# The weights of the modulation in groups of eight units at every hand-over, two of them ahead of the sums of squares, and the copies that end a group behind later products

## The chip, the cores and the metric

One core of a Trainium2 chip runs the whole program. The metric is the device time of one execution in microseconds; a kernel's time is the median of its runs.

## What is computed

One inference step of a decoder trunk of four layers (width D = 1024, feed-forward width 2816), in float32. 256 prompt tokens and 8 samples of 4 tokens each use the same weights, so the matrices work on 288 columns. The modulation vectors come from the conditions alone (one for the prompt, eight for the samples), so that they can be computed at any time before they are needed:

```
c_act = silu(c)
for i in range(4):                                  # mixers: pool, attention, GLA, pool
    shift1, scale1, gate1, shift2, scale2, gate2 = split(c_act @ w_ada[i] + b_ada[i], 6)
    h = rms_norm(x, norm_gain[i, 0]) * (1 + scale1) + shift1
    x = x + gate1 * mixer(h)                        # mixer i mod 3, with its state or caches
    h = rms_norm(x, norm_gain[i, 1]) * (1 + scale2) + shift2
    x = x + gate2 * conv_ffn(h)                     # up-projection, width-3 conv, gelu gate, down-projection
y = rms_norm(x, final_gain)
```

The pool mixer subtracts tokens from their causal windowed means and multiplies four groups by their own matrices; the attention mixer has three dilation groups merged by their denominators; GLA is gated linear attention in chunks of 64. States and caches are outputs too.

## The kernel before

Activations lie transposed, features on partitions and the 288 tokens on the free axis, in eight tiles of 128 features. A product in float32 is made of three matmuls (`prod`, L386 to L390): weights and activations are each split into a high and a low half, and high x high (L388), high x low (L389) and low x high (L390) are summed in PSUM. The weights are split on the chip: ScalarE copies a half unit into `whi` (L320), VectorE subtracts that from the raw weights into `wlo` (L328).

**Steps and loads.** The whole program is one list of steps, executed by `execute` (L257). A step with a `piece` is a product on half a unit of weights; the splits of its piece are placed ahead of it, up to four pieces (`W_BUFS`), or `ahead` pieces where a step says so. A step with a `unit` reads raw weights. Units are 1 MB (128 x 2048 float32). They are loaded by SyncE (L299) in the order of their use into a ring of six raw buffers (`RAW_BUFS`); a new load is issued when a buffer comes free, that is after the last `wlo` of a weight unit or after the matmuls of a modulation unit. `lows`, the pending `wlo` subtractions, are emitted behind the next step.

**Modulation** (`ada_steps`, L487 to L543). `w_ada` of one layer is 24 units of 1 MB. A group makes two vectors out of eight units, or one vector out of four (`groups` says which: first vector, number). A unit is eight matmuls of 128x512 on the 32 columns of the conditions (L508), summed in one PSUM tile of its own (`adaps`). Behind the last unit of a group come two "busy" steps: `evac`, a copy of that PSUM tile by ScalarE to `adasb` (L518), and `fin`, four transposes on TensorE (ps<-cm,adasb in the rows, by the helper at L384) and the additions on VectorE (L529, L537). Layer 0's units stand in the start of the program and in its mixer. Layers 1 to 3 are computed out of a queue, some of it a layer ahead.

**Where the queue is drained.** The mixers' steps stand in strings written out by hand (`POOL_ORDERS`, `ATTN_ORDER`, `GLA_ORDER`); a "+" is the next step of the queue, be it a unit, an `evac` or a `fin`. In the FFNs `place` (L196) puts units after counted pieces, by `FFN_FILL`: so many units where the first norm is, and then `{piece: units}`. Its `ends` lets the busy steps stand one piece or more behind the last unit. `arrange` (L1961) reads the strings.

**A hand-over.** At the end of each mixer and each FFN the last weight pieces give the eight feature tiles of the residual. `each` (L581) adds a tile into `x` (L596, L598, L600), ScalarE squares it (L556), VectorE adds squares up in `ssq` (L559), and after the last tile two matmuls against a matrix of ones give the sums over the features (`square_add`, L570; sqps<-ssq and sqps<-sq). Then the root (L609 to L616) and the norm, which writes the halves `hh` and `hl` of the next input (L648, L679, L684) that the next products wait for. The modulation units of the hand-over (six of them at most places: `norm + + + + + +`, `begin + + + + + +`) stand between the sums and those products in TensorE's order. In the pool mixer the products are L981 to L983, the means' transposition L1018 to L1022, and its residual has names of its own (`add0`, `squares0`, `add1`, `squares1`).

At the attention layer kr0 transposes probabilities (ps<-cm,P), o-steps accumulate values (acc<-kv,PT), mx and om merge the groups, and w0a to w3b are the output products, with O as what is merged. In GLA fi0 to fi3 make the halves of the output (L1850 to L1852), and w0a to w3b are its output products.

Of the kernel before, what the change touches and what calls it, by code (L numbers as in the profile page):

```python
# [44 lines left out]
norm + + + + + + norm2 gates product0 product1 + + pre ys0 ys1 + + add0 squares0 add1 squares1 end  # L45
# [4 lines left out]
+ + + t0a y1a v0a t0d y1b v0b o0a kr0 t0c s1a y1c wr0 q2a o0b o0c sv0 t1a + + y1d s1b q2b t1b s1c y1e o0d k2a  # L50
y1f y1g s1d k2b t1c t1d + + kr1 v1a y1h sc1 + v1b s2a v2a o1a t2a o1c o1b st1 s2b v2b y2a t2b o1d y2b sv1 sc2
s2c s2d kr2 + wt mu0 om1 t2d mu1 wr2 om0 st2 o2a wr1 mx0 sm1 o2b t2c sm0 mx1 w0a sv2 om2 o2c o2d w1a sm2 mx2 pre + +
+ w0b + w1b + w3a w2a w2b w3b end
# [3 lines left out]
begin + + + + + + q0a q0b gd masks q1a + ga2 ga0 q1b ga1 + k0a cu0 + k0b cu3 k1a cu2 cu1 k1b xs6 xs5 es x0 v0a  # L57
ms5 x1 ks v0b ms7 m0b + m0a v1a x2 ms6 m1a m1b ps m2a up0 v1b v2a x3 uo0 un0a un0c m3a un0b m3b x4 up1 m2b un0d
v2b uo1 m4b v3a un1b x5 m4a + un1a m5a m5b x6 un1c up2 v3b m6a un1d uo2 + un2a m7a m6b un2c r0a en cr kr0 m7b un2b +
un2d r0b kr1 op1 r1a op0 up3 uo3 un3a un3c r1b un3b un3d r2a os op3 op2 sp0 ns0 sp1 si0 ns1 nr0 og1 r2b r3a ns2 ns3 og0 nr1  # L60
r3b fi0 fi1 si1 og2 og3 + pre + + w0a + w1a + fi2 fi3 + + w0b w1b w2a w2b w3a w3b end
"""

FFN_FILL = ((0, {8: 4, 20: 4, 34: 4}), (6, {30: 2}), (6, {16: 2, 34: 4}), (4, {}))
# [106 lines left out]
class Step:  # L171


    __slots__ = ("fn", "piece", "unit", "gap", "busy", "ahead", "key", "need")
# [21 lines left out]
def place(main, queue, first, runs):  # L196


    out, ends = [], []
    queue = list(queue)  # L200
    seen = 0

    def units(n):
        while n:
            s = queue.pop(0)
            n -= not s.busy
            (ends if s.busy else out).append(s)
            if s.busy and len(ends) > 2:
                out.append(ends.pop(0))
        while queue and queue[0].busy:  # L210
            ends.append(queue.pop(0))
    for s in main:
        if s.need is not None:
            if queue and queue[0].key <= s.need:
                raise ValueError(f"late: {queue[0].key}")
            out.append(s)
            units(first)
            continue
        out.append(s)
        if s.piece is not None:  # L220
            seen += 1
            if ends:
                out.append(ends.pop(0))
            if seen in runs:
                units(runs[seen])
    return out, queue


class Trunk:
# [27 lines left out]
    def execute(self, steps):  # L257
# [53 lines left out]
        for kind, v in plan:  # L311
# [20 lines left out]
            else:  # L332
# [154 lines left out]
    def ada_steps(self, l, m0, nm, own=None):  # L487
# [53 lines left out]
        for s in st:  # L541
            s.key = (l, m0)
# [34 lines left out]
    def residuals(self, i, m):  # L577

        sq = [self.ssq]

        def each(t, ps):  # L581
            f, G = 2 * i + t, m()
            if f == 7:
                self.flush(self.adds)
            self.residual_x(ps, f, G)
            self.flush(self.adds)
            sq.append(self.square(f, "later"))
            if f == 7:
                self.square_add(6, self.ssq)
                self.square_add(7, sq[-1])  # L590
        return each
# [482 lines left out]
    def attn_steps(self, l):  # L1074
# [418 lines left out]
        for i in range(4):  # L1493
            put(f"w{i}", self.pair_steps(w_out[:, i * 256:(i + 1) * 256], lambda: (self.hh, self.hl), None, (6,), ((0, 4), (4, 6)),
                                         each=self.residuals(i, lambda: self.mod(l, 2)), ahead=AHEAD if i == 3 else None))
        return T
# [394 lines left out]
    def build(self):  # L1891
# [6 lines left out]
        for n, l in enumerate(Ls):  # L1898
            groups = ((0, 2), (2, 1), (4, 1), (3, 1), (5, 1)) if n == 0 else ((0, 2), (2, 1), (3, 2), (5, 1)) if n == len(Ls) - 1 else ((0, 2), (2, 2), (4, 2))
# [14 lines left out]
        for n, l in enumerate(Ls):  # L1914
            kind = l % 3
            after = None
            if kind == 0:
                if n == 0:
# [3 lines left out]
                    p["product0"].ahead, p["product1"].ahead = 2, 1  # L1922
# [4 lines left out]
                p["pre"] = Step(lambda: self.preload(AF.Abs_reciprocal_sqrt), ahead=None if n else 2)  # L1927
                after = p.pop("outs2")
                m = self.arrange(p, POOL_ORDERS[min(n, 1)], queue)
            else:  # L1930
                m = m2 if kind == 1 else self.gla_steps(l)
                m = self.arrange(m, ATTN_ORDER if kind == 1 else GLA_ORDER, queue)
# [12 lines left out]
            f, queue = place(f, queue, *FFN_FILL[n])  # L1945
# [5 lines left out]
    def arrange(self, named, order, queue):  # L1951

        out = []
        for t in order.split():
            if t != "+":
                s = named.pop(t)
                while s.need is not None and queue and queue[0].key <= s.need:
                    out.append(queue.pop(0))
                out.append(s)
            elif queue:  # L1960
                out.append(queue.pop(0))  # L1961
# [94 lines left out]
```

## Time and profile before

| | |
|---|---|
| median of three runs | 1398.32 us (1393.46, 1398.32, 1399.51) |
| the profiled execution | 1400.07 us |
| its span | 1398.3 us |
| mean granted clock of TensorE | 0.973 |
| HBM read and written | 300.21 MB and 19.76 MB |
| DMA rate over the span | 229 GB/s |

The span is what the profiler saw from the first to the last instruction; the execution's time has 1.8 us more around it. In the page's lines a row is a group of instructions: line, engine, operation, output<-inputs, shapes, number, then busy us and mean ns of one, and behind a second bar the idle time ahead of them and what ended it. DVE is VectorE, ACT ScalarE, POOL GpSimd, SP SyncE, PE TensorE, PEld its loading of weights.

### The profile page before, as it was taken

What the parts mean: (1) busy time and instruction counts of PE and PEld (TensorE: products, weight loads), DVE (VectorE), ACT (ScalarE), POOL (GpSimd) and SP (SyncE); (2) the same over time, 40 slices, a digit from 0 to 9 for tenths busy, and PEclk for the clock granted to TensorE, in tenths of its full rate; (3) what the DMA queues carried; (4) which work ended last, traced back from release to release, by engine and by line L of the source; (5) the groups of instructions that cost most, each with busy time, mean ns of one, the idle gap of its engine ahead of it and who ended that gap; (6) DMA issues with size and microseconds to landing.
All of it is one profiled execution on the core that took longest, in us unless ns stands there. A gap on an engine that the chain in (4) does not pass through costs nothing.

```text
span 1398.3 us, 25411 instructions
## 1 busy us (share of the span) xinstructions
PE 1330.4 (95%) x10075; PEld 1205.3 (86%) x10075; DVE 853.2 (61%) x1673; ACT 641.4 (46%) x1152; POOL 209.4 (15%) x510
## 2 busy tenths in 40 slices
PE   5899999998999999999999999799999999999997
PEld 3479899987786699999978887699999967999997
DVE  2576666446335776674465654676765566777644
ACT  3364445335443555453354336364544344545542
POOL 2220011001001122110034324121100021101100
PEclk8899999999999999999999999999999997999999
DMA  9997866559656796875593476596575577545520
GB/s 344 356 301 267 263 205 218 173 181 341 229 188 215 276 315 228 289 266 172 181 339 101 151 241 223 192 314 232 181 246 173 172 286 239 166 158 165 174 84 34
DMA packets 206231, 310.48 MB, mean 222 GB/s; under 512 B 7692, under 2 KB 186742, under 8 KB 196496
## 3 DMA queue, kind: packets, MB, share of 16 engines
q1 hardware_dynamic: 201296, 286.82, 61.3%
q0 software_dynamic: 4352, 21.50, 4.2%
q8 instruction: 79, 1.29, 0.4%
q10 hardware_dynamic: 464, 0.54, 0.1%
q14 instruction: 40, 0.33, 0.1%
HBM read 300.21 MB, written 19.76 MB: 229 GB/s over the span
## 4 chain that ended last, share of the span: by engine, by line
PE 83%; DVE 6%; DMA 4%; ACT 3%; issue 2%; POOL 1%; SPq 0%; DVEq 0%; ACTq 0%; POOLq 0%
PE mm L388 22%; PE mm L390 22%; PE mm L389 22%; PE adaps L508 4%; DMA raw<-w_ada 3%; PE ps L384 2%; DMA raw<-attn_w_in 1%; PE ps L1625 1%; PE sqps L570 1%; PE mm L758 1%; PE mm L759 1%; PE mm L760 1%; DVE ht L648 1%; DVE hl L684 1%; DVE wlo L328 1%
## 5 line engine op out<-in xcount | busy, mean ns | idle before, releaser
L388 PE MATMUL mm<-hh,whi 128*128 128x288 f32 (+1 forms) x1752 | 524.4, 299 | 3.4 <-ACT hh L679 1.9
L389 PE MATMUL mm<-hl,whi 128*128 128x288 f32 (+1 forms) x1752 | 519.3, 296 | 0.8 <-DVE hl L684 0.6
L390 PE MATMUL mm<-hh,wlo 128*128 128x288 f32 (+1 forms) x1752 | 519.2, 296 | 0.1
L328 DVE TENSOR_TENSOR wlo<-raw,whi 128x1024 fp32r<-128x1024 f32 (+2 forms) x335 | 393.3, 1190 | 152.5 <-ACT whi L320 152.1
L320 ACT ACTIVATE whi<-raw 128x1024 fp32r<-128x1024 f32 (+2 forms) x335 | 343.0, 1028 | 281.5 <-PE mm L389 184.8
L388 PEld LDWEIGHTS mm<-hh,whi 128*128 128x128 f32 (+1 forms) x1752 | 330.9, 189 | 17.0 <-issue 9.2
L389 PEld LDWEIGHTS mm<-hl,whi 128*128 128x128 f32 (+1 forms) x1752 | 330.8, 189 | 1.9 <-POOL hs L671 0.6
L390 PEld LDWEIGHTS mm<-hh,wlo 128*128 128x128 f32 (+1 forms) x1752 | 330.6, 189 | 0.6 <-DVE wlo L328 0.3
L388 PE MATMUL mm<-ah,whi 128*128 128x288 f32 x704 | 208.5, 296 | 0.0
L390 PE MATMUL mm<-ah,wlo 128*128 128x288 f32 x704 | 208.0, 295 | 0.0
L389 PE MATMUL mm<-al,whi 128*128 128x288 f32 x704 | 206.9, 294 | 0.0
L389 PEld LDWEIGHTS mm<-al,whi 128*128 128x128 f32 x704 | 132.8, 189 | 0.0
L388 PEld LDWEIGHTS mm<-ah,whi 128*128 128x128 f32 x704 | 132.5, 188 | 0.0
L390 PEld LDWEIGHTS mm<-ah,wlo 128*128 128x128 f32 x704 | 132.3, 188 | 0.0
L815 DVE TENSOR_SCALAR c<-ext,vec 128x304 f32<-128x304 f32 x88 | 38.7, 439 | 127.3 <-ACT ext L812 124.9
L818 DVE SCALAR_TENSOR_TENSOR c<-ext,vec,c 128x304 f32<-128x304 f32 x176 | 94.9, 539 | 6.3
L508 PE MATMUL adaps<-raw,cT 128*32 128x512 f32 x736 | 92.7, 631 | 5.8 <-DMA raw<-w_ada 5.8
L824 POOL COPY convS<-ext 128x2 f32<-128x2 f32 x88 | 16.2, 184 | 448.7 <-ACT ext L811 448.7
L811 ACT ACTIVATE ext<-mm 128x256 f32<-128x256 f32 x88 | 33.9, 386 | 83.0 <-PE mm L390 83.0
L821 ACT ACTIVATE ge<-c 128x304 f32<-128x304 f32 x88 | 39.9, 458 | 57.4 <-DVE c L818 56.6
L508 PEld LDWEIGHTS adaps<-raw,cT 128*32 128x32 f32 x736 | 20.6, 112 | 52.9 <-issue 39.7
L556 ACT ACTIVATE sq<-x 128x288 f32<-128x288 f32 x63 | 27.7, 444 | 63.5 <-DVE x L600 56.0
(387 smaller groups left out, 1484.6 us busy)
## 6 DMA issues: line engine op xcount, KB each, us to landing
raw<-w_ada SPq DMA_DIRECT2D x92, 1024.0 KB, 5.8
raw<-ffn_w_in SPq DMA_DIRECT2D x80, 1024.0 KB, 8.7
raw<-ffn_w_down SPq DMA_DIRECT2D x32, 1024.0 KB, 5.0
raw<-ffn_w_down SPq DMA_DIRECT2D x16, 768.0 KB, 6.1
raw<-gla_w_in SPq DMA_DIRECT2D x12, 1024.0 KB, 13.4
raw<-ffn_w_in SPq DMA_DIRECT2D x16, 512.0 KB, 6.2
win_s<-cache_win_g POOLq DMA_DIRECT2D x16, 512.0 KB, 4.6
raw<-attn_w_in SPq DMA_DIRECT2D x7, 1024.0 KB
```

The costliest lines, as they stand in the source:

```text
L320: self.nc.scalar.activation(out=hv, in_=r, func=AF.Copy)
L328: self.nc.vector.tensor_tensor(out=lv, in0=r, in1=hv.bitcast(F32), op=ALU.subtract)
L384: self.nc.tensor.transpose(out=out, in_=in_, identity=self.ident[0:k, 0:k])
L388: mmul(out=out, lhsT=wh, rhs=xh, start=start, stop=False)
L389: mmul(out=out, lhsT=wh, rhs=xl, start=False, stop=False)
L390: mmul(out=out, lhsT=wl, rhs=xh, start=False, stop=stop)
L508: nc.tensor.matmul(out=ps[32 * q:32 * q + 32, :], lhsT=self.cT[:, k * per + r, :], rhs=v[:, r, j * 512:(j + 1) * 512], start=(k == 0), sto ...
L556: nc.scalar.activation(out=sq, in_=self.x[:, f, :], func=AF.Square)
L811: nc.scalar.activation(out=e[:, 2:258], in_=ps[t][:, 0:TP], func=AF.Copy)
L815: nc.vector.tensor_scalar(out=c1, in0=e[:, 0:304], scalar1=w[0], scalar2=self.vcol("ffn_conv_b", l * 22 + f), op0=ALU.mult, op1=ALU.add)
L818: nc.vector.scalar_tensor_tensor(out=c1, in0=e[:, k:k + 304], scalar=w[k], in1=c1, op0=ALU.mult, op1=ALU.add)
L821: nc.scalar.activation(out=ge, in_=c1, func=AF.Gelu)
```

## The change

`place` goes, and with it the drawing of units, `evac` and `fin` by separate "+". The new `spread` only puts "+" marks behind counted pieces of an FFN, and the new `fill` goes through the finished list: a "+" takes one unit. When the last unit of a group is taken, its `evac` is put three pieces further on and its `fin` five pieces further on, or ahead of the next group's first unit or of the step that needs the vectors, whichever comes first.

At every hand-over from layer 1 on there are two units ahead of the sums of squares, which are now a step of their own (`self.sums`), and six behind: a whole group of eight. At the last one, into FFN3, four units are left, two ahead of the second half of the sums' steps and two behind. The units in the FFNs of layers 1 to 3 go; in attention and GLA pairs stand at four places each (in attention after kr0, y1g, st1 and o2a; in GLA after x4, pre, w0a and fi3). In layer 3 the order of the groups becomes (0,2), (3,2), (2,1), (5,1), two units stand behind the pool products, and `gates` (which needs the vector of the gate) moves behind the products. Three of attention's steps and the pool's products and `pre` in layer 3 get a smaller `ahead`. The number of units, and every sum, stays. Buffers stay at six. At f == 7 the residual is now added ahead of the pending adds, and the pending `wlo` are emitted ahead of a unit's load.

```
+def spread(main, runs):
+    out = []
+    seen = 0
+    for s in main:
+        out.append(s)
+        if s.piece is not None:
+            seen += 1
+            out.extend("+" * runs.get(seen, 0))
+    return out
+
+def fill(entries, queue):
     out, ends = [], []
     queue = list(queue)
     seen = 0
+    def take():
+        s = queue.pop(0)
+        if s.first:
+            while ends:
+                out.append(ends.pop(0)[1])
+        out.append(s)
+        k = 3
         while queue and queue[0].busy:
+            ends.append((seen + k, queue.pop(0)))
+            k += 2
+    for e in entries:
+        if e == "+":
+            if queue:
+                take()
             continue
+        if e.need is not None:
+            while any(q.key <= e.need for q in queue):
+                take()
+            while any(q.key <= e.need for _, q in ends):
+                out.append(ends.pop(0)[1])
+        out.append(e)
+        if e.piece is not None:
             seen += 1
+            while ends and ends[0][0] <= seen:
+                out.append(ends.pop(0)[1])
...
-norm + + + + + + norm2 gates product0 product1 + + pre ys0 ys1 + + add0 squares0 add1 squares1 end
+norm + + + + + + norm2 product0 product1 + + gates pre ys0 ys1 add0 squares0 add1 + + squares1 end
...
-FFN_FILL = ((0, {8: 4, 20: 4, 34: 4}), (6, {30: 2}), (6, {16: 2, 34: 4}), (4, {}))
+FFN_RUNS = ({8: 4, 20: 4, 34: 4}, {}, {}, {})
...
                     v.fn(*[u.view(raw.pop(u)) for u in v.unit])
+                    flush_lows()
                     for u in v.unit:
...
             f, G = 2 * i + t, m()
-            if f == 7:
-                self.flush(self.adds)
             self.residual_x(ps, f, G)
             self.flush(self.adds)
             sq.append(self.square(f, "later"))
             if f == 7:
-                self.square_add(6, self.ssq)
-                self.square_add(7, sq[-1])
+                def sums():
+                    self.square_add(6, self.ssq)
+                    self.square_add(7, sq[-1])
+                self.sums = sums
...
+            if n and kind == 0:
+                f = list("++") + [f[0]] + list("+" * 6) + f[1:]
+            elif n:
+                f = ["+", "+", Step(lambda: self.sums()), f[0]] + list("+" * 6) + f[1:]
+            if n:
+                m = ["+", "+", Step(lambda: self.sums())] + m
             st += m + f
-        return st
+        return fill(st, queue)
```

How it moves TensorE's instructions at the hand-over from FFN1 to GLA: the last rows of the down-projection (al and ah are its input's halves), the sums, the units (a row of 4 is one unit) and GLA's first product. Before:

```order
L388 MATMUL mm<-ah,whi 128x288
L389 MATMUL mm<-al,whi 128x288
L390 MATMUL mm<-ah,wlo 128x288
L570 MATMUL sqps<-ssq,ones 128x288
L570 MATMUL sqps<-sq,ones 128x288
L508 MATMUL adaps<-raw,cT 32x512 x24
L388 MATMUL mm<-hh,whi 128x288
```

and now, at the same place of the changed kernel, whose lines are some 16 further down:

```order
L404 MATMUL mm<-ah,whi 128x288
L405 MATMUL mm<-al,whi 128x288
L406 MATMUL mm<-ah,wlo 128x288
L524 MATMUL adaps<-raw,cT 32x512 x8
L586 MATMUL sqps<-ssq,ones 128x288
L586 MATMUL sqps<-sq,ones 128x288
L524 MATMUL adaps<-raw,cT 32x512 x24
L404 MATMUL mm<-hh,whi 128x288
```

Two units moved ahead of the two sums, and six are still behind them.

The loads that SyncE issues for that place, in order, before:

```order
L299 DMA raw<-gla_w_in 128x8x256
L299 DMA raw<-w_ada 128x2048 x6
L299 DMA raw<-gla_w_in 128x8x16
L299 DMA raw<-gla_w_in 128x8x256 x2
L299 DMA raw<-w_ada 128x2048
L299 DMA raw<-gla_w_in 128x8x256
```

and now:

```order
L314 DMA raw<-gla_w_in 128x8x256
L314 DMA raw<-w_ada 128x2048 x8
L314 DMA raw<-gla_w_in 128x8x16
L314 DMA raw<-gla_w_in 128x8x256 x7
L314 DMA raw<-state_gla 128x8x256
L314 DMA raw<-w_ada 128x2048 x2
```

Eight loads of w_ada now stand ahead of GLA's next weights, where six stood, and the units that were spread over GLA's start are no longer between its weights.

In attention, on TensorE around kr0 (kT keys, P probabilities and cm the constant used for transposing), before:

```order
L1268 MATMUL acc<-kv,PT 128x64
L384 MATMUL ps<-cm,kT 128x128 x4
L384 MATMUL ps<-cm,kT 32x128 x2
L384 MATMUL ps<-cm,P 128x128 x3
L1227 MATMUL ps<-kT,qT 128x128
```

and now:

```order
L1284 MATMUL acc<-kv,PT 128x64
L400 MATMUL ps<-cm,kT 128x128 x4
L400 MATMUL ps<-cm,kT 32x128 x2
L524 MATMUL adaps<-raw,cT 32x512 x8
L400 MATMUL ps<-cm,P 128x128 x3
L1243 MATMUL ps<-kT,qT 128x128
```

Two units stand between the transposition of the keys and that of the probabilities.

More of the change, by code (lines that the diff above doesn't have):

```diff
@@ L171 @@
 class Step:
-    __slots__ = ("fn", "piece", "unit", "gap", "busy", "ahead", "key", "need")
+    __slots__ = ("fn", "piece", "unit", "gap", "busy", "ahead", "key", "need", "first")
     def __init__(self, fn, piece=None, unit=None, gap=0, busy=False, ahead=None, need=None):
@@ L193, in merge @@
     return out
-def place(main, queue, first, runs):
+def spread(main, runs):
[8 more added lines that the diff above has]
+def fill(entries, queue):
     out, ends = [], []
@@ L201, in place @@
     seen = 0
[L203 to L209, printed above, removed]
-        while queue and queue[0].busy:
[L211 to L217, printed above, removed]
-            continue
-        out.append(s)
-        if s.piece is not None:
-            seen += 1
[L222 to L226, printed above, removed]
+    def take():
[5 more added lines that the diff above has]
+        k = 3
+        while queue and queue[0].busy:
+            ends.append((seen + k, queue.pop(0)))
[4 more added lines that the diff above has]
+                take()
+            continue
+        if e.need is not None:
[5 more added lines that the diff above has]
+        if e.piece is not None:
+            seen += 1
+            while ends and ends[0][0] <= seen:
+                out.append(ends.pop(0)[1])
+    if queue or ends:
+        raise ValueError("units left")
+    return out
 class Trunk:
@@ L540, in ada_steps @@
         st.append(Step(fin, busy=True))
-        for s in st:
-            s.key = (l, m0)
+        for k, s in enumerate(st):
+            s.key, s.first = (l, m0), k == 0
         return st
@@ L1495, in attn_steps @@
                                          each=self.residuals(i, lambda: self.mod(l, 2)), ahead=AHEAD if i == 3 else None))
+        for t in ("v1b", "v2a", "v2b"):
+            T[t].ahead = 2
         return T
@@ L1921, in build @@
                             p[f"b{k}{i}"] = step
-                    p["product0"].ahead, p["product1"].ahead = 2, 1
                     p["root"] = Step(self.root)
@@ L1926, in build @@
                     del p["open"], p["past"], p["room"]
-                p["pre"] = Step(lambda: self.preload(AF.Abs_reciprocal_sqrt), ahead=None if n else 2)
+                p["product0"].ahead, p["product1"].ahead = 2, 1
+                p["pre"] = Step(lambda: self.preload(AF.Abs_reciprocal_sqrt), ahead=2)
                 after = p.pop("outs2")
-                m = self.arrange(p, POOL_ORDERS[min(n, 1)], queue)
+                m = self.arrange(p, POOL_ORDERS[min(n, 1)])
             else:
                 m = m2 if kind == 1 else self.gla_steps(l)
-                m = self.arrange(m, ATTN_ORDER if kind == 1 else GLA_ORDER, queue)
+                m = self.arrange(m, ATTN_ORDER if kind == 1 else GLA_ORDER)
             f = self.ffn_steps(l)
@@ L1944, in build, with arrange @@
                 f.insert(24, m2.pop("lines"))
-            f, queue = place(f, queue, *FFN_FILL[n])
+            f = spread(f, FFN_RUNS[n])
             if kind == 1:
                 f = merge(f, self.copies, 8, len(f) - 26)
-            st += m + f
-        return st
[L1951 to L1961, printed above, removed]
+            if n and kind == 0:
[4 more added lines that the diff above has]
+                m = ["+", "+", Step(lambda: self.sums())] + m
+            st += m + f
+        return fill(st, queue)
+    def arrange(self, named, order):
+        out = [t if t == "+" else named.pop(t) for t in order.split()]
         if named:
```

18 lines of the change are left out of this document (9 added, 9 removed).

## The prediction

> **What bounds the kernel now.** I read the page first: the span, the busy time of the engines, the costliest groups and the DMA issues.
>
> ```profile
> span 1398.3 us, 25411 instructions
> PE 1330.4 (95%) x10075; PEld 1205.3 (86%) x10075; DVE 853.2 (61%) x1673; ACT 641.4 (46%) x1152; POOL 209.4 (15%) x510
> L508 PE MATMUL adaps<-raw,cT 128*32 128x512 f32 x736 | 92.7, 631 | 5.8 <-DMA raw<-w_ada 5.8
> raw<-w_ada SPq DMA_DIRECT2D x92, 1024.0 KB, 5.8
> ```
>
> TensorE is busy 95% of the span, so only two things can move the end: its idle time, some 68 us, and the clock at which it works. The modulation units (L508, 8 matmuls each) are work that can stand anywhere, and a unit's megabyte takes a median of 5.8 us from issue to landing. Next I read TensorE's waits (total, times, longest).
>
> ```profile
> PE ps L384 <- DVE hl L1852: 7.7, 1, 7.7
> PE sqps L570 <- DVE ssq L559: 4.3, 5, 2.5
> PE sqps L570 <- ACT sq L556: 1.7, 5, 0.4
> PE ps L384 <- DVE kv L1205: 1.4, 1, 1.4
> PE ps L384 <- DVE O L1418: 1.1, 1, 1.1
> PE ps L1227 <- ACT KT L1305: 0.7, 1, 0.7
> PE ps L1227 <- ACT PT L1254: 0.5, 1, 0.5
> ```
>
> The largest is at the end of GLA. The two waits of the sums of squares come to 4.3 + 1.7 = 6.0 us. The other four are in attention. Third, the timeline of TensorE at the hand-over from FFN1 to GLA (start, length, idle before in brackets), and SyncE's issues there.
>
> ```profile
> 696.15 0.75 PE L570 MATMUL sqps<-ssq,ones 128*128 128x288 f32 x2 [0.55 <-DVE ssq L559]
> 697.22 0.75 PE L570 MATMUL sqps<-sq,ones 128*128 128x288 f32 x2 [0.31 <-ACT sq L556]
> 697.90 5.36 PE L508 MATMUL adaps<-raw,cT 128*32 128x512 f32 x48
> 703.19 0.40 PE L388 MATMUL mm<-hh,whi 128*128 128x288 f32 x1
> ```
>
> ```profile
> 693.07 0.33 SPq L299 DMA_DIRECT2D raw<-w_ada  x1
> 699.02 2.94 SPq L299 DMA_DIRECT2D raw<-gla_w_in  x3
> ```
>
> Six units run for 5.36 us without a gap while the norm is made, and the first product follows at once. All six were loaded beforehand; the next load is issued at 699.02, that is 1.12 us after the first unit began, when its buffer is free. Last, the windows view, for the clock (columns: from and to, length, busy time of PE, PEld, DVE, ACT, POOL, then PEclk, DMA share, GB/s).
>
> ```profile
> 365.86:369.27 3.41, 2.02 (x16) 1.56 (x16) 2.48 (x4) 0.59 (x2) 0.39 (x1) 1.00 0.03 9
> 369.27:372.68 3.41, 3.41 (x15) 2.76 (x14) 0.81 (x5) 1.82 (x7) 1.54 (x3) 0.50 0.46 175
> 471.67:475.08 3.41, 1.56 (x8) 0.72 (x12) 2.24 (x8) 0.90 (x3) 0.00 (x0) 1.00 0.73 238
> 475.08:478.50 3.42, 3.42 (x20) 0.88 (x21) 2.43 (x9) 1.62 (x5) 1.28 (x4) 0.50 0.22 87
> ```
>
> A stretch of 3.41 us in which TensorE was idle for 3.41 - 2.02 = 1.39 us is followed by one at half clock, and so is one with 1.85 us idle. Such a stretch costs half its length, 1.7 us, if it is filled with work. So waits that fall together into one window are dearer than they look.
>
> **The change part by part**, against the profiled execution.
>
> 1. *Units moved.* A unit costs 5.36/6 = 0.89 us of TensorE wherever it stands, and their number stays. 0.
>
> 2. *Two units ahead of the sums.* At five hand-overs (into attention, FFN1, GLA, FFN2 and the pool layer) the last products are followed by 1.7 us of units, which hide the residual, the square and the add of the last feature. The longest wait is the 2.5 at FFN1, of which 2.5 - 1.7 = 0.8 stays, with 0.4 for the square behind it 1.2. -6.0 + 1.2 = **-4.8**. The sums themselves wait in TensorE's queue behind the two units, so the norm starts up to 1.7 - 0.9 us later at GLA; six units still stand behind it, as before.
>
> 3. *Eight units on six buffers.* The seventh load goes out when the first unit's buffer is free. With T0 for the first unit's start that is T0 + 1.1, and with 5.8 to landing T0 + 6.9. TensorE is there at T0 + 1.7 (two units) + 1.4 (two sums at 0.7) + 3.4 (four units) = T0 + 6.5: a wait of 0.4. For the eighth, the spacing of units that are limited by their transfers shows in the pool layer.
>
> ```profile
> 1145.10 1.07 PE L508 MATMUL adaps<-raw,cT 128*32 128x512 f32 x8 [0.26 <-DMA raw<-w_ada]
> 1147.60 1.07 PE L508 MATMUL adaps<-raw,cT 128*32 128x512 f32 x8 [1.44 <-DMA raw<-w_ada]
> ```
>
> They are 2.5 us apart, so the eighth lands at T0 + 9.4, where TensorE, after the seventh, is ready at T0 + 7.8: 1.6. Together 2.0 at most at each hand-over; nothing at the least, if a lone megabyte lands faster than the median. I take 1.6, nearer to the median row than to none, at five places: **+8.0** (0 to 10).
> By the Trainium skill ("DMA: Bandwidth & Descriptors", Anatomy of one DMA — SWDGE (gpsimd) path), a transfer has a fixed part of about 2.0 us. That and the 2.5 us from the row make 4.5, an estimate by which the last unit would wait 0.7 and the term be +3.5; the median row of 5.8 speaks against it, yet includes transfers in company.
>
> 4. *Loads behind the units.* The next stage's first transfers go out two loads later. At the start of attention one is already late, beside a full DMA:
>
> ```profile
> 319.83 1.09 PE L384 MATMUL ps<-cm,raw 128*128 128x128 f32 x8 [2.48 <-DMA raw<-cache_win_g]
> 318.07:321.48 3.41, 1.65 (x14) 1.65 (x15) 3.41 (x10) 2.04 (x4) 3.41 (x7) 1.00 1.09 360
> ```
>
> It moves from seventh to ninth, 5 us later at 2.5 each, while TensorE comes 2 x 0.89 plus the waits of item 3 plus the 1.4 of the sums later, about 4.8. **+1.0** (0 to 2) with the small loads at the two FFNs.
>
> 5. *Clock.* Item 3 lays up to 2.0 us idle into 3 us, above the 1.39 that was followed by half clock, but a window's edge can split it. I take two of five hand-overs: +3.4. FFN1's half-clock window is there already:
>
> ```profile
> 474.96 7.05 PE L508 MATMUL adaps<-raw,cT 128*32 128x512 f32 x48
> ```
>
> These six units take 7.05 - 5.36 = 1.7 us more than at GLA. The idle 1.85 that came before goes with item 2: -1.7. The one at 369.27 in attention goes with a unit pair at kr0: -1.7. Behind the attention merge a new one is as likely as not (item 6): +0.85. Sum **+0.85** (-3.4 to +6.8).
> The Trainium skill ("TensorE: Matmul & The Clock Gate", What's actually happening) halves the clock after at least one idle window of about 3.4 us; the rows above do it after 1.39 us, so the trace disagrees, and the rule is a rival below.
>
> 6. *Attention.* Pairs now cover the four waits of 1.4, 1.1, 0.7 and 0.5 us: -3.7. Where single units went, waits open. At the merge three units stood (start, length) behind which the first output product waited for nothing:
>
> ```profile
> 454.16 2.78 PE L508 MATMUL adaps<-raw,cT 128*32 128x512 f32 x24
> 455.29 0.42 DVE L1437 TENSOR_TENSOR hl<-ps,hh 128x256 fp32r<-128x256 f32 x1 [0.18 <-ACT hh L1436]
> ```
>
> Without them TensorE is ready at 454.2 for a low half that ends at 455.7: 1.5. For three further places I take 0.5 each, the least of the four waits above. -3.7 + 3.0 = **-0.7** (-3.7 to +2).
>
> 7. *GLA's end.*
>
> ```profile
> 876.63 0.82 DVE L1852 TENSOR_TENSOR hl<-o,hh 128x288 fp32r<-128x288 f32 x1 [0.51 <-ACT hh L1851]
> 880.99 0.46 DVE L1852 TENSOR_TENSOR hl<-o,hh 128x288 fp32r<-128x288 f32 x1 [0.51 <-ACT hh L1851]
> 881.50 1.11 PE L384 MATMUL ps<-cm,adasb 128*128 128x128 f32 x4 [7.67 <-DVE hl L1852]
> ```
>
> A modulation copy stands first in TensorE's order and waits 7.67 us for DVE, whose low halves come one every 1.3 us from 876.6 to 881.4. Put behind later products, it lets w0b start on halves that are there; but the last of them still ends at 881.4, and the units that stood in between go to other places, so little is left to run. I take -1.5 of the 7.67. Units taken from the earlier part leave one unit's length, 0.9, open. **-0.6** (-4 to +2).
>
> 8. *Pool layer.*
>
> ```profile
> 1155.27 1.12 PE L384 MATMUL ps<-cm,adasb 128*128 128x128 f32 x4 [1.72 <-ACT adasb L518]
> 1150.92:1167.99 17.07, 15.35 (x64) 14.18 (x64) 11.18 (x28) 6.90 (x16) 0.00 (x0) 0.50 0.60 203
> 1169.02 3.64 PE L508 MATMUL adaps<-raw,cT 128*32 128x512 f32 x32
> 1172.50 0.80 DVE L684 SCALAR_TENSOR_TENSOR hl<-ht,modT,hh 128x256 fp32r<-128x256 f32 x1 [0.44 <-ACT hh L679]
> ```
>
> 1.72 + 1.44 + 0.26 = 3.4 us of waits go; the two units left behind the products are late by about 2.6: -0.8. At FFN3 four units of 3.64 cover the norm just so, its first low half ending at 1173.3, and two are now left: +1.7. The half clock of 1150.92 to 1167.99 stays. **+0.9** (-2 to +2).
>
> Sum: 0 - 4.8 + 8.0 + 1.0 + 0.85 - 0.7 - 0.6 + 0.9 = +4.65. The profiled execution took 1400.07 us, 1.75 more than the median of the three runs shown (1398.32), so it would come to 1404.7; on the median's scale 1403.0. What a measurement here can tell from no change is about half a per cent, 7 us: below 1391.3 or above 1405.3.
>
> **The rivals.** *The seventh and eighth land in time.* Then items 3 and 4 and the new half clocks (8.0 + 1.0 + 3.4 + 0.85 = 13.25) are gone: 4.65 - 13.25 = -8.6, so 1389.7. For it: the DMA rows at the hand-over show 87 GB/s at 475, a nearly empty queue, so a lone load may beat the median. Against it: units 2.5 us apart at 1145. Chance 0.28, of which 0.20 faster and 0.08 same.
>
> *Half clock at every hand-over* (slower). If the 2.0 us of item 3 fall into one window at all five, three more windows at 1.7 (+5.1) and the half chance made whole (+0.85) give +10.6: 1408.9. It decides at about 1.4 us idle in a window. Against it: the windows run freely, so some edge should split them. Chance 0.15.
>
> *No half clock follows the new waits*, because they are two short ones: 4.65 - 4.25 = +0.4, so 1398.7. The skill's rule named in item 5 would give this. Against it stand the 1.39 us. Chance 0.11, same.
>
> That the change does not do all it says: the last hand-over, FFN3's, gets four units and not eight, since no more are left; that is in item 8.
>
> **How the numbers follow.** The main case has 0.46; by the bounds of items 4 to 8 its own range is 1396 to 1409, of which 0.31 lies within half a per cent and 0.15 above. Faster 0.20; same 0.31 + 0.08 + 0.11 = 0.50; slower 0.15 + 0.15 = 0.30. The range goes from 1388, below the first rival, to 1412, above the second with the ring's waits at 10 instead of 8.
>
> **What would show it.** In the new waits of TensorE: "sqps <- ssq" below 1.3 us in all; "adaps <- raw<-w_ada" up from 5.8 to some 12, at the seventh and eighth unit of each hand-over; half-clock windows behind these units; the wait of 7.67 gone from the copy and found again, shorter, at w0b; about 1.5 us at the first product after FFN3's two units. I am wrong if the w_ada waits stay under 5 us (then it is faster), or if GLA gives back most of 7.67.

## The result and the profile after

The changed kernel takes 1414.81 us (median of four runs, 1411.46 to 1421.08) against 1395.89 for the kernel before in the same measurement: a ratio of 1.0141, 95% interval 1.0093 to 1.0189. It is slower by about 19 us. The forecast was 1403.0, the range ended at 1412. The profiled execution took 1413.89 us against 1400.07, 13.8 us more; that is what the two traces can account for.

The page of the changed kernel, the rows that answer to those of before (L508 is now L524, L570 is L586, L384 is L400):

```profile
span 1412.1 us, 25410 instructions
PE 1342.7 (95%) x10075; PEld 1212.2 (86%) x10075; DVE 850.7 (60%) x1673; ACT 641.5 (45%) x1152; POOL 207.6 (15%) x510
L524 PE MATMUL adaps<-raw,cT 128*32 128x512 f32 x736 | 95.2, 641 | 15.1 <-DMA raw<-w_ada 15.1
```

Span less busy time is TensorE's idle time: 69.4 us after, 67.9 before. So idle time grew by 1.5 us only, while the same 10075 matmuls took 12.3 us longer. In the windows of 3.41 us at half clock TensorE was busy for 63.6 us before and for 85.1 us after; half of the difference, 10.7 us, is an estimate of what half clock cost in addition. So the kernel became slower less by waiting than by working at half clock, and a wait matters by what it sets off.

The windows view by stage says where (each row begins at the end of one stage's last product and ends at that of the next, so a hand-over's units lie in the stage behind it; columns as before, the clock is the third number from the end). Before, the attention, GLA, FFN2 and pool stages:

```profile
309.70:470.69 160.99, 150.34 (x1377) 122.01 (x1376) 82.65 (x239) 70.33 (x161) 13.31 (x25) 0.98 0.72 249
...
695.60:902.75 207.15, 189.47 (x1373) 160.37 (x1372) 122.06 (x219) 93.45 (x160) 68.61 (x93) 0.94 0.61 210
902.75:1130.07 227.32, 226.62 (x1717) 217.06 (x1716) 147.12 (x264) 109.12 (x186) 23.53 (x80) 1.00 0.67 215
1130.07:1164.81 34.74, 30.02 (x193) 22.72 (x194) 26.33 (x61) 15.62 (x32) 7.82 (x19) 0.80 0.82 297
```

and after:

```profile
310.92:477.83 166.91, 155.79 (x1380) 124.64 (x1384) 82.81 (x239) 70.21 (x160) 13.30 (x25) 0.94 0.70 240
...
703.39:916.10 212.71, 196.53 (x1377) 164.49 (x1380) 118.98 (x218) 93.72 (x160) 68.10 (x93) 0.92 0.60 205
916.10:1141.74 225.64, 223.42 (x1684) 217.11 (x1688) 146.85 (x260) 108.78 (x185) 23.52 (x80) 0.99 0.62 197
1141.74:1176.95 35.21, 30.91 (x232) 21.34 (x236) 24.57 (x63) 14.18 (x31) 7.80 (x19) 0.90 1.02 376
```

Attention is 5.9 us longer at a clock of 0.94 instead of 0.98, GLA 5.6 us at 0.92 instead of 0.94, both with about the same number of units. FFN2 and pool together are 1.2 us shorter. The other stages make up the remaining 3.5 us, FFN3 1.7 of it.

**In attention** the timeline of ScalarE, after:

```profile
426.95 1.06 ACT L335 ACTIVATE whi<-raw 128x1024 fp32r<-128x1024 f32 x1 [3.59 <-DMA raw<-attn_w_out]
...
428.97 0.60 ACT L1321 ACTIVATE KT<-ps 128x512 f32<-128x512 f32 x1
```

and TensorE and SyncE in the same place:

```profile
418.62 1.92 PE L524 MATMUL adaps<-raw,cT 128*32 128x512 f32 x16
...
429.62 1.11 PE L400 MATMUL ps<-cm,raw 64*128 64x64 f32 x8 [2.53 <-ACT KT L1321]
430.66 1.93 PE L1396 MATMUL ps<-raw,PTs 128*32 128x256 f32 x16
```

```profile
420.60 10.54 SPq L314 DMA_DIRECT2D raw<-attn_w_out  x2
```

Read in order: the pair of units at st1 ends at 420.5 and frees its buffers; only then, at 420.60, is the first load of attn_w_out issued. ScalarE's split of it comes next in its queue and waits 3.59 us, to 426.95. The copies of the values and then of the keys (L1321) stand behind it in the same queue, though their own data are there. TensorE waits 2.53 us for the keys. The windows from there on:

```profile
425.55:428.97 3.42, 1.54 (x17) 1.33 (x14) 0.00 (x0) 1.98 (x4) 0.00 (x0) 1.00 0.20 65
428.97:432.38 3.41, 2.76 (x24) 1.52 (x24) 2.23 (x3) 1.47 (x3) 0.00 (x0) 0.50 0.12 26
432.38:435.79 3.41, 3.41 (x32) 0.99 (x32) 0.42 (x1) 0.00 (x0) 0.00 (x0) 0.50 0.59 205
435.79:439.21 3.42, 3.42 (x95) 2.74 (x87) 1.92 (x5) 0.36 (x2) 0.00 (x0) 0.50 0.39 99
439.21:442.62 3.41, 2.68 (x12) 1.41 (x9) 2.45 (x12) 1.97 (x10) 0.00 (x0) 0.50 0.41 100
442.62:446.03 3.41, 3.41 (x19) 2.49 (x23) 3.21 (x17) 0.85 (x3) 1.35 (x1) 0.50 0.54 190
```

One window with 1.88 us idle, then five at half clock, 17 us. In two of the first three of these TensorE is busy without a gap, and the clock still does not come back. The matmuls there are thin ones: on 32 columns or rows in the first of the two, on 32 or 64 in the second.

**At the hand-overs** the two FFN1 units that wait, and GLA's:

```profile
486.27 1.06 PE L524 MATMUL adaps<-raw,cT 128*32 128x512 f32 x8 [0.88 <-DMA raw<-w_ada]
488.97 1.06 PE L524 MATMUL adaps<-raw,cT 128*32 128x512 f32 x8 [1.64 <-DMA raw<-w_ada]
```

```profile
706.34 4.50 PE L524 MATMUL adaps<-raw,cT 128*32 128x512 f32 x40
713.63 1.07 PE L524 MATMUL adaps<-raw,cT 128*32 128x512 f32 x8 [2.79 <-DMA raw<-w_ada]
```

They are the seventh and eighth of their group at FFN1, the eighth at GLA. The eighth waits at all five hand-overs, the seventh only at FFN1 and in the pool layer. The sums, on the other hand, wait 0.9 us in all, as against 6.0:

```profile
PE adaps L524 <- DMA raw<-w_ada: 15.1, 11, 2.8
...
PE ps L1810 <- DVE PT L1618: 3.5, 2, 3.0
...
PE ps L400 <- ACT KT L1321: 2.5, 1, 2.5
...
PE sqps L586 <- DVE ssq L575: 0.9, 1, 0.9
```

**At GLA's end** the wait of 7.7 us is gone from the list. The windows of the two kernels there, before and then after:

```profile
874.44:877.86 3.42, 0.00 (x0) 0.00 (x0) 2.19 (x4) 0.45 (x2) 3.42 (x4) 1.00 1.00 413
877.86:881.27 3.41, 0.00 (x0) 0.00 (x0) 1.93 (x5) 1.63 (x4) 0.38 (x5) 0.50 1.01 418
881.27:884.69 3.42, 3.19 (x14) 3.19 (x15) 0.83 (x6) 0.17 (x1) 0.00 (x0) 0.50 0.87 355
```

```profile
889.77:893.18 3.41, 1.89 (x9) 0.90 (x6) 2.39 (x5) 0.89 (x2) 2.58 (x7) 1.00 1.08 390
893.18:896.59 3.41, 3.24 (x10) 2.14 (x10) 1.90 (x5) 1.83 (x3) 0.00 (x0) 0.50 1.02 423
896.59:900.01 3.42, 3.42 (x16) 3.42 (x16) 1.91 (x7) 0.44 (x1) 0.00 (x0) 0.50 1.00 395
```

Before, the first of two half-clock windows fell on idle time and cost nothing; after, 1.52 us of idle time is followed by two that are nearly full of products. What is left of the gain is small: from the first product on grr (L1847, now L1865) to the stage's end it is 41.6 us instead of 42.8, with 52 matmuls of units in it instead of 40.

GLA's loss lies ahead of that. The first product comes 11.2 us after the stage's start instead of 7.6, behind two units more and the wait of 2.8 us. And the stretch from the first to the last of the products ps<-X (L1636 and L1625, now L1654 and L1643), with two units in it in both kernels, takes 3.4 us more at a lower clock, before and then after:

```profile
746.70:810.71 64.01, 56.27 (x454) 49.85 (x454) 42.88 (x73) 23.00 (x36) 25.46 (x38) 0.91 0.39 132
```

```profile
757.84:825.25 67.41, 59.05 (x450) 51.66 (x450) 40.14 (x68) 23.01 (x36) 25.45 (x38) 0.85 0.39 126
```

### The profile page after: what moved, and what is told of

Same layout as the page of the kernel before. It is cut to its first block, busy times and chain, and to the rows that moved or that the text cites. A ratio compares the mean times of both kernels' runs of the same rounds, so it can differ in the third digit from the quotient of the medians.

```text
span 1412.1 us, 25410 instructions
## 1 busy us (share of the span) xinstructions
PE 1342.7 (95%) x10075; PEld 1212.2 (86%) x10075; DVE 850.7 (60%) x1673; ACT 641.5 (45%) x1152; POOL 207.6 (15%) x510
## 4 chain that ended last, share of the span: by engine, by line
PE 83%; DVE 5%; DMA 5%; ACT 3%; issue 2%; POOL 1%; SPq 1%; DVEq 0%; ACTq 0%; POOLq 0%
PE mm L404 22%; PE mm L406 22%; PE mm L405 22%; PE adaps L524 4%; PE ps L400 2%; DMA raw<-w_ada 1%; PE ps L1643 1%; DMA raw<-attn_w_in 1%; DMA raw<-state_ffn_conv 1%; PE mm L774 1%; DMA own<-x_prompt 1%; SPq L314 1%; PE mm L775 1%; PE mm L776 1%; DVE ht L664 1%
## 5 line engine op out<-in xcount | busy, mean ns | idle before, releaser
L524 PE MATMUL adaps<-raw,cT 128*32 128x512 f32 x736 | 95.2, 641 | 15.1 <-DMA raw<-w_ada 15.1
L524 PEld LDWEIGHTS adaps<-raw,cT 128*32 128x32 f32 x736 | 20.2, 113 | 66.2 <-issue 36.3
```

The source lines that it names most:

```text
L524: nc.tensor.matmul(out=ps[32 * q:32 * q + 32, :], lhsT=self.cT[:, k * per + r, :], rhs=v[:, r, j * 512:(j + 1) * 512], start=(k == 0), sto ...
```

## The experiments

The theory had three parts: the seventh and eighth unit of a hand-over wait for buffers and set off half clock; attention's pair at st1 delays attn_w_out, with the chain above; GLA's extra time comes from where units and copies stand in it. The rivals stand in each expectation. Ratios are to the kernel before, with their 95% intervals.

**six_hand.** Two of the eight units go ahead of the stage's end (in attention ahead of w2b, in GLA of w3a), six stay behind the sums.

```
-FFN_RUNS = ({8: 4, 20: 4, 34: 4}, {}, {}, {})
+FFN_RUNS = ({8: 4, 20: 4, 34: 4, 64: 2}, {64: 2}, {64: 2}, {})
-w0b w1b w3a w2a w2b w3b end
+w0b w1b w3a w2a + + w2b w3b end
...
-                m = ["+", "+", Step(lambda: self.sums())] + m
+                m = [Step(lambda: self.sums())] + m
```

> Of each hand-over's eight units, two stand two to four weight pieces ahead of the stage's end, none ahead of the sums and six behind them, as in the kernel before; all else as changed. Theory (eight units on six buffers make the waits of the seventh and eighth unit, 15.1 us of w_ada waits against 5.8 before, and the half-clock windows that follow them): the w_ada waits fall to about 6 us, the sums' waits come back to about 6, and some 8 us of the 18.9 lost are given back, so about 1407. Rival (the loss lies in attention and GLA alone): w_ada waits fall but the sums' waits take their place, 1413 to 1416.

1409.63 us, 1.0082 (1.0057 to 1.0107). Its waits:

```profile
PE sqps L586 <- DVE ssq L575: 6.2, 5, 1.6
...
PE adaps L524 <- DMA raw<-w_ada: 4.0, 4, 2.1
```

As the theory had it: w_ada's waits fall from 15.1 to 4.0 us, the sums' come back. FFN1, without any half clock now, takes 222.2 us instead of 225.6. GLA stays at 212.8. The interval still touches that of the changed kernel (1.0093 to 1.0189), so the waits and the stage show this step better than the time.

**two_four.** The same, but two units stay ahead of the sums and four behind (the six of the strings and lists become four).

> As the run before it in two units standing ahead of the stage's end, but two units stay ahead of the sums and only four behind them. Theory of the ring: w_ada waits about 6 us, sums' waits about 1; the norm is now covered by four units (3.4 us) where six stood, so each hand-over waits about 1.5 us for its first high or low half: 5 x 1.5 = 7.5. Sum -9 + 7.5, so about 1413, and slower than the run with six behind the sums. Rival (the norm needs no more than four units): 1405.

1405.63 us, 1.0059 (1.0032 to 1.0085), outside the interval of the changed kernel. Its profiled execution was the slowest of its runs, 1416.04 us. The expectation was wrong on the norm: the first products behind four units wait less than 1.5 us.

```profile
PE mm L406 <- DVE wlo L343: 2.0, 3, 0.7
...
PE mm L405 <- DVE hl L700: 1.7, 5, 0.5
```

In the changed kernel these two are 0.5 and 0.8 us, and the products' wait for hl in the pool layer (L998) rises from 1.6 to 2.7: some 3.5 us more over five hand-overs, not 7.5. So four units cover the norm nearly as six do.

**zero_eight.** All eight behind the sums (in the mixers' strings too).

```
-                f = ["+", "+", Step(lambda: self.sums()), f[0]] + list("+" * 6) + f[1:]
+                f = [Step(lambda: self.sums()), f[0], "+", "+"] + list("+" * 6) + f[1:]
```

> All eight units of each of the five hand-overs stand behind the sums, none ahead of them; all else as changed. If the two units ahead hide the sums' waits as predicted, these come back (0.9 to about 6 us); the seventh and eighth unit are reached 1.4 us earlier or not at all later, so the w_ada waits stay at 13 to 16 us: about 1419. Rival (the two ahead gain nothing, because what they hide is paid again at the seventh and eighth unit): 1413 to 1415, with sums' waits of 6 and w_ada waits of 10.

1427.33 us, 1.0203 (1.0175 to 1.0230), worse than expected. Both waits are there at once:

```profile
PE adaps L524 <- DMA raw<-w_ada: 19.5, 13, 3.3
PE sqps L586 <- DVE ssq L575: 7.3, 5, 2.8
```

Against six_hand, which also has none ahead, the two units more in the burst cost 1.2%. The rival, which had 1413 to 1415 us and 10 us of waits for w_ada, falls: the two ahead of the sums gain even with a ring that is too short. Against the changed kernel the intervals just touch (1.0175 and 1.0189).

One stretch goes the other way. GLA behind its hand-over has the same order as in the changed kernel, but the products ps<-X take 4.6 us less, at a clock of 0.92:

```profile
766.55:829.32 62.77, 54.83 (x449) 48.90 (x449) 42.72 (x68) 23.14 (x36) 25.48 (x38) 0.92 0.44 136
```

So the order in GLA's middle does not by itself make it slow.

**pair_early.** Attention's pair leaves st1.

```
-y1f y1g + + s1d k2b t1c t1d kr1 v1a y1h sc1 v1b s2a v2a o1a t2a o1c o1b st1 + + s2b v2b
+y1f y1g + + s1d k2b t1c t1d kr1 v1a y1h sc1 + + v1b s2a v2a o1a t2a o1c o1b st1 s2b v2b
```

> The pair of units at st1 in attention stands at sc1, some 14 us earlier; all else as changed. Theory (the load of attn_w_out waits for the buffer that this pair holds, lands late, ScalarE stands 3.6 us at the split of it with the keys' copy behind, TensorE waits 2.5, and five windows of half clock follow): ScalarE's wait for attn_w_out and the wait for KT are below 0.5 us, the half clock from 429 to 446 us is gone or one window, attention is shorter by 7 to 8 us and the kernel about 1407. Rival (the thin matmuls of the merge bring the half clock whatever is waited for): the KT wait goes, the half clock stays, 2.5 us, about 1412.

1407.52 us, 1.0057 (1.0036 to 1.0078), also outside the interval of the changed kernel. ScalarE's split no longer waits, and TensorE's matmuls follow at once:

```profile
420.79 1.04 ACT L335 ACTIVATE whi<-raw 128x1024 fp32r<-128x1024 f32 x1
...
423.56 0.60 ACT L1321 ACTIVATE KT<-ps 128x512 f32<-128x512 f32 x1
```

```profile
424.55 0.71 PE L400 MATMUL ps<-cm,raw 64*128 64x64 f32 x8
425.18 1.07 PE L1396 MATMUL ps<-raw,PTs 128*32 128x256 f32 x16
```

Attention takes 159.8 us, 7.1 less. The rival falls here: the same sixteen thin matmuls (L1396) take 1.07 us instead of 1.93. They don't bring the half clock here; they only failed to end it there.

**split_late.** The pair stays at st1, and ScalarE's split moves behind the copies that it held up.

```
-        for t in ("v1b", "v2a", "v2b"):
-            T[t].ahead = 2
+        for t, k in (("v1b", 2), ("v2a", 2), ("v2b", 1), ("sv1", 2)):
+            T[t].ahead = k
```

> Attention's pair of units stays at st1, but ScalarE's split of attn_w_out's first half, which stood ahead of the copies of v2b and of the keys, stands behind them (at sv1); all else as changed. Theory (it is the in-order queue of ScalarE, in which the split waits 3.6 us for the late attn_w_out, that holds back the keys and with them TensorE, and half clock follows): the wait for KT is below 0.5 us, the half clock from 429 to 446 us is gone or one window, attention shorter by 6 to 8 us, kernel about 1407, as with the pair moved. Rival (moving the pair helped by standing at sc1, not by the split): attention within 2 us of the changed kernel's 166.9, kernel 1413 to 1415.

1409.66 us, 1.0074 (1.0055 to 1.0093). Attention takes 162.9 us, 4 less and not 6 to 8: the wait for the keys is gone, and one of 2.2 us for the softmax's maximum (Ms, L1348) opened a little later, with two windows of half clock. So the queue of ScalarE is the link of the chain, as the theory says, and this order only moves the split in front of something else.

**gla_spread.** Single units at or near their old places in GLA.

```
-ms5 x1 ks v0b ms7 m0b m0a v1a x2 ms6 m1a m1b ps m2a up0 v1b v2a x3 uo0 un0a un0c m3a un0b m3b x4 + + up1 m2b un0d
-v2b uo1 m4b v3a un1b x5 m4a un1a m5a m5b x6 un1c up2 v3b m6a un1d uo2 un2a m7a m6b un2c r0a en cr kr0 m7b un2b
+ms5 x1 ks v0b ms7 m0b m0a v1a x2 ms6 m1a m1b ps m2a up0 v1b v2a x3 uo0 un0a un0c m3a un0b m3b x4 + up1 m2b un0d
+v2b uo1 m4b v3a un1b x5 m4a + un1a m5a m5b x6 un1c up2 v3b m6a un1d uo2 + un2a m7a m6b un2c r0a en cr kr0 m7b un2b +
...
-r3b fi0 fi1 si1 og2 og3 pre + + w0a + + w1a fi2 fi3 + + w0b w1b w2a w2b w3a w3b end
+r3b fi0 fi1 si1 og2 og3 pre + + w0a + w1a + fi2 fi3 w0b w1b w2a w2b w3a w3b end
```

> GLA's eight units behind the hand-over stand as one after x4, m4a, uo2, un2b, w0a and w1a and two after pre, near where they stood before, instead of four pairs after x4, pre, w0a and fi3. Theory (the pairs left VectorE's waits in GLA's middle uncovered: 2.0 and 3.0 us and the half-clock windows behind them): the stretch from 780 to 840 us is shorter by about 4 us; the end may lose 1 to 2 of this where no pair stands behind fi3: about 1412. Rival (the half clock in GLA's middle is as before and only shifted): no change within 1 us, or slower by the 1.7 at the end.

1415.05 us, 1.0108 (1.0074 to 1.0143), not told apart from the changed kernel. GLA takes 213.1 us, as against 212.7. Two waits in its middle are back at their old size (2.0 us at L1810, 1.2 at L1643), but w0b, without the pair behind fi3, now waits 2.8 us for its high half. The rival's number is right.

**copies_early.** The copies stand one and two pieces behind the last unit, not three and five.

```
-        k = 3
+        k = 1
...
-            k += 2
+            k += 1
```

> The copy that ends a group of units stands one piece behind its last unit and the transposes two pieces, instead of three and five; all else as changed. Theory (their place matters little: TensorE's waits for adasb are 3.7 us after against 3.2 before, and the pool layer's alone are new): within 3 us of the changed kernel. Rival (the late place is what shortened GLA's end by some 3 us and the early one brings the wait of 7.7 back): 1417 to 1419.

1415.62 us, 1.0113 (1.0088 to 1.0138), GLA 213.6 us. The time does not tell this place of the copies from the changed kernel's, and the 7.7 us at GLA's end don't come back with it.

**old_places.** All units where they stood before; the rest as changed (some ten places in the strings, `FFN_RUNS` with {30: 2} and {16: 2, 34: 4}, no units ahead of the sums).

> The units stand where they stood before (six behind each hand-over's sums and none ahead, singles and pairs in attention and GLA, runs in FFN1 and FFN2), while the later copies, the order of layer 3's groups, the gates behind the products and the smaller split distances stay as changed. Theory (all of the loss is the units' places; the rest gains about 3 us at GLA's end, where 7.7 of wait went and half clock took most of it, and up to 3 in the pool layer): 1393 to 1397, same as or a little faster than before. Rival (the later copies or the split distances cost in the mixers): 1403 or more.

1406.26 us, 1.0047 (1.0025 to 1.0069), so the expectation was missed. Attention is back at 160.9 us and FFN1 at 223.4. But two waits stand out as new:

```profile
PE ps L400 <- ACT adasb L534: 9.7, 4, 7.5
...
PE ps L400 <- DVE modT L545: 2.8, 1, 2.8
```

The 7.5 us are in the pool layer, and they are the same kind of chain as attention's. With the old places and the new order of layer 3's groups, a group ends among the units behind the sums, and its copy comes behind the norm in ScalarE's queue: the last of eight copies of the norm (L695) and then the units' (L534).

```profile
1146.37 0.51 ACT L695 ACTIVATE hh<-ht,modT 128x256 fp32r<-128x256 f32 x1 [0.28 <-DVE ht L664]
1146.79 0.58 ACT L534 ACTIVATE adasb<-adaps 128x512 f32<-128x512 f32 x1
```

The four units had ended at 1139.9; the stage takes 41.5 us. The 2.8 us are in GLA, where a transposition (ps<-cm,Ke) waits for VectorE's additions (modT) that end a group and that the count of pieces now puts ahead of it. So the new order of groups and the counted places don't fit the units' old places, and the run does not separate what they cost in the changed kernel.

**combo.** two_four and pair_early together.

> The changed kernel with the two causes found so far undone together: the hand-overs' eight units as two ahead of the stage's end, two ahead of the sums and four behind (as in two_four), and attention's pair at sc1 instead of st1 (as in pair_early). Theory (ring and attention are separate and add up): two_four stood at 1.0059 of before and pair_early took about 0.7% off the changed kernel, so 0.999 to 1.001 of before, about 1398; GLA stays 3 to 5 us longer than before. Rival (both take the same half-clock loss away): 1.004 to 1.006, about 1405.

1400.46 us, 1.0023 (1.0004 to 1.0041). They add up to most of what was lost; a little less than expected, more than the rival. Attention takes 156.3 us, GLA 213.2.

**combo_gla.** Units and copies of GLA behind the hand-over at their old places.

```
-begin + + + + q0a q0b gd masks q1a ga2 ga0 q1b ga1 k0a cu0 k0b cu3 k1a cu2 cu1 k1b xs6 xs5 es x0 v0a
+( begin + + + + q0a q0b gd masks q1a ga2 ga0 q1b ga1 k0a cu0 - k0b cu3 k1a cu2 cu1 k1b xs6 xs5 es x0 v0a
...
-r3b fi0 fi1 si1 og2 og3 pre + + w0a + + w1a fi2 fi3 + + w0b w1b w2a w2b + + w3a w3b end
+r3b fi0 fi1 si1 og2 og3 + pre + + w0a + w1a + fi2 fi3 - - ) w0b w1b w2a w2b + + w3a w3b end
...
+                hold[0] = 1000 if e == "(" else 0
```

(a "-" is the next copy, and between the brackets none is placed by counting).

> As combo, and in GLA the units behind the hand-over stand one by one at the places that they had before (m4a, uo2, un2b, og3, two at pre, w0a, w1a) and the copies that end groups at their old places too (evac behind cu0 and fin behind m0b; both behind fi3). Theory (GLA's extra 4 us come from where units and copies stand in its thin stretch and at its end): GLA comes back to some 205 to 207 us with 14 units in it, and the kernel is 3 to 4 us below combo, 0.997 of before. Rival (GLA's extra time is where the free-running clock windows fall): within 1.5 us of combo.

1397.74 us, 1.0007 (0.9982 to 1.0031). In its profile GLA takes 209.9 us, 3.4 less than in combo and not the 205 to 207 expected, and the 7.7 us of wait are back. The intervals of the two kernels overlap, and the trace does not settle it either: combo and two_four have the same order in GLA, and there it took 213.2 and 210.1 us. Over all profiles GLA took 207.2 to 209.4 us in the four kernels that leave its order behind the hand-over as before, and 210.1 to 213.6 in the eight that keep the changed four pairs; so the places probably count, but the rival is not ruled out.

**before_one.** The kernel before, with one unit of six ahead of the sums at five hand-overs and five behind.

```
-begin + + + + + + q0a
++ sums begin + + + + + q0a
...
```

> The kernel before with one of the six units of each of five hand-overs moved ahead of the sums and five left behind; nothing else. The sums' waits are 6.0 us, most of them below a unit's 0.89, so about 5 go. Theory (the norm needs all six units: two_four's gain at the sums was lost again at its first products): the first products behind five units wait 0.5 to 1 us each, so the kernel is within 2 us of before, 0.999 to 1.001. Rival (the first part of the change is good by itself): 0.996, 5 us faster.

1393.11 us, 0.9969 (0.9944 to 0.9993): the rival is right, the first idea of the change is good by itself, with one unit. The sums wait 1.9 us instead of 6.0, and the first products don't pay it back.

**before_two.** The same with two ahead and four behind.

> The kernel before with two of the six units of each of five hand-overs ahead of the sums and four behind; nothing else. before_one (one and five) stood at 0.997. The sums' waits, 1.5 us there, go to below 1; the first products behind four units wait some 0.5 to 1 us each more for the norm's halves. Theory (one unit is enough for the sums, the second is missed behind them): 1.000 to 1.002, 4 us behind before_one. Rival (the second unit is worth what the prediction gave it, its cover of the 2.5 us at FFN1): 0.995 to 0.997.

1395.04 us, 0.9966 (0.9947 to 0.9985). The second unit shows neither gain nor loss; the theory of the norm's cover is wrong again, as in two_four.

**best.** before_one, and attention's ten units behind the hand-over as pairs at kr0, y1g, sc1, o2a and pre, with the changed split distances.

```
+t0a y1a v0a t0d y1b v0b o0a kr0 + + t0c s1a + y1c wr0 q2a + o0b o0c sv0 t1a y1d s1b q2b t1b s1c y1e o0d k2a
+y1f y1g + + s1d k2b t1c t1d kr1 v1a y1h sc1 + + v1b s2a v2a o1a t2a o1c o1b st1 s2b v2b y2a t2b o1d y2b sv1 sc2
+s2c s2d kr2 wt mu0 om1 t2d mu1 wr2 om0 st2 o2a + + wr1 mx0 sm1 o2b t2c sm0 mx1 w0a sv2 om2 o2c o2d w1a sm2 mx2 pre + +
+w0b + w1b + w3a w2a w2b w3b end
```

> before_one with attention's ten units behind the hand-over as five pairs, at kr0, y1g, sc1, o2a and pre, and the smaller split distances of the changed kernel, the copies at s1a, q2a, w0b and w1b; nothing else. In combo attention with pairs at kr0, y1g, sc1 and o2a took 156.3 us where before had 161.0 and before_one 159.3. Theory (the pairs in attention gain by themselves, as the prediction's item 6 had it, and only the one at st1 lost): attention 156 to 157, 0.994 to 0.995 of before, 1390 to 1391. Rival (combo's short attention came from how the clock's windows fell): attention 159 to 161, 0.997.

1391.92 us, 0.9947 (0.9928 to 0.9966), as the theory had it and faster than both kernels. The interval overlaps that of before_one, so what the pairs add shows in the stage rather than in the time:

```profile
313.33:469.27 155.94, 149.03 (x1381) 119.91 (x1384) 82.51 (x239) 69.64 (x160) 13.31 (x25) 1.00 0.75 257
```

No half clock is left in it, and it is 5 us shorter than before and 3.4 shorter than in before_one (159.3).

## Why the prediction was wrong

It forecast +4.65 us, within half a per cent; it was +13.8 in the profiles and 1.4% in the medians. Step by step:

- **The step that failed in attention is item 6, with item 5 behind it.** Item 6 saw what the pairs cover in attention and listed waits that could open on TensorE; it did not follow the pair's two buffers to the load that comes after them in SyncE's order, nor that load to ScalarE's queue. pair_early shows it: moving that one pair takes 7.1 us off attention. The hand-over's 1.6 of item 3 and the -0.7 of item 6 made +0.9 us for this stage; it was +5.9.
- **Item 5 priced a fall of the clock at one window.** "Such a stretch costs half its length, 1.7 us" held at the three hand-overs where the clock fell; in attention, where thin matmuls follow, it lasted five windows, and at GLA's end two, though wide products follow there. The page of before had the sign of it: 17 us at half clock in the pool layer, in a row that the prediction quotes and only carries along as unchanged. (It did not stay: after, it is three windows, 10 us.) At the hand-overs the count of two new windows was right (into attention and FFN2), but FFN1's old one did not go.
- **Item 3 had the mechanism and was mis-sized.** The waits for w_ada at the five hand-overs are 2.3, 2.5, 2.8, 2.0 and 2.0 us, 11.6 in all, against 8.0 taken and 10 as the end. The seventh unit, taken to wait 0.4 everywhere, waits only at FFN1 (0.9) and in the pool layer (0.6). By the Trainium skill's fixed part of a transfer (DMA: Bandwidth & Descriptors, Anatomy of one DMA — SWDGE (gpsimd) path) the prediction had an estimate of 0.7 each; the waits here are three times that. The Trainium skill gives that figure for transfers on GpSimd's path, and these loads are issued by SyncE.
- **Item 2 was right**: 6.0 to 0.9 us, -5.1 against -4.8. before_one shows a gain of 0.3% from one unit ahead where nothing else is changed, before_two one as large from two.
- **Item 7 was wrong.** The wait of 7.67 us went almost wholly, not by 1.5, but half clock on full windows took most of the gain, and the end is 1.2 us shorter. In GLA's middle the item took one open wait of 0.9; the products ps<-X there take 3.4 us more, with waits of 2.0 and 3.0 us (L1643 and L1810 for PT) where 1.2 and 2.0 had been and with more half clock, and ahead of them la is waited for 2.1 us instead of 0.8. -0.6 was forecast and the stage is 5.6 us longer, of which the hand-over has its 2.8 less the sums' 0.9: a miss nearly as large as attention's. Why the middle is longer stays open: zero_eight, with the same order there, took 62.8 us, less than the 64.0 of before, and neither gla_spread nor combo_gla settles it.
- **Item 8 was right in FFN3** (+1.7 of the stage). Item 4's +1.0 did not come: cache_win_g's wait is 1.9 us instead of 2.5, and the small loads at the FFNs wait 0.5.

Of the rivals, the first falls: the eighth unit came late at all five hand-overs, the seventh at two. The slower one came nearer in time than the forecast, but not by its mechanism, for only three hand-overs of five are followed by half clock. The third falls with those three; the rule of the Trainium skill behind it (TensorE: Matmul & The Clock Gate, What's actually happening), an idle window of about 3.4 us, does not hold in this trace, where 1.52 us idle in a window was followed by half clock.

## What to carry to other kernels

Be wary of a burst of filler work that is longer than the ring of its buffers: here the eighth unit on six buffers waited 1.5 to 2.8 us at every hand-over. When a step that holds buffers is moved, follow the buffers: to the next load in the order of issue, to the instruction that waits for that load, and to everything that stands behind it in that engine's queue. And price a wait by the work that follows it: at this kernel's hand-overs it cost itself and at most one slow window, ahead of attention's thin matmuls it cost five.

## What the runs showed of the hardware

In the changed kernel ten of the fourteen windows of 3.41 us at full clock with 1.5 us or more of idle time were followed by a granted clock of 0.50. There was no sharp sill: 1.01 us was enough once, 1.50 was not another time (the second of these rows was followed by 0.50, the first by 1.00).

```profile
736.17:739.58 3.41, 1.91 (x15) 1.72 (x13) 1.08 (x2) 2.16 (x3) 0.73 (x1) 1.00 0.44 141
783.95:787.37 3.42, 2.41 (x23) 1.84 (x15) 2.94 (x7) 0.00 (x0) 0.00 (x0) 1.00 0.65 195
```

Idle time is not all that counts. In the pool layer a window without any was followed by three at 0.50; most of its matmuls (ys<-dd, L1020, L1021 and L1023) have only 32 or 64 columns of moving data. The kernel before shows the same at 1147.51, with 0.09 us idle.

```profile
1166.25:1169.66 3.41, 3.41 (x32) 3.41 (x32) 2.58 (x4) 0.84 (x3) 0.00 (x0) 1.00 1.01 402
```

Once down, the clock stayed at 0.50 in attention through a window that TensorE filled without a gap with matmuls on 32 columns or rows (432.38 to 435.79); the same matmuls ran through at 1.00 in pair_early, where the clock had not gone down before them. In the pool layer it stayed down through full windows of matmuls with weights of 128 x 128 as well (L1034 to L1038, 1169.66 to 1176.49), so thin weights are not the whole of it, and what the clock goes by is not shown here.
